# A causal mask added by the vector engine instead of a matmul, a third slot for split weights and six gate buffers

## The chip, the cores and the metric

The kernel runs on one NeuronCore of a Trainium2 chip. A core has a matrix engine (PE in the profile; PEld is its weight load), a vector engine (DVE), a scalar engine (ACT), a second elementwise engine (POOL, GpSimd) and SyncE (SP, which only issues DMAs here). Each engine takes its instructions strictly in the order in which they stand in its stream; between engines there are semaphores. SBUF is the large on-chip memory, PSUM the eight banks into which matmuls write. The metric is the device time of one launch in microseconds (us).

## The reference, cut to what matters

One layer of a streaming encoder: a new stream of 1024 frames ("prompt") and 32 further frames of a running stream ("sample"). The input is normalised and projected to q, k, v, a forget gate, the conv inputs and four gates (ga, gb, ma, mb). One branch is causal softmax attention in 16 heads of 64 channels with a bias from cumulative forget gates, the other a causal depthwise convolution of width 31 with a LayerNorm.

```python
def fox_attend(q, k, v, cq, ck, qpos, kpos):
    s = jnp.einsum('bqhd,bkhd->bhqk', q, k)
    bias = cq[..., None] - ck[:, None, :]              # per head, C = cumsum(log f)
    mask = qpos[:, None] >= kpos[None, :]
    s = jnp.where(mask[None, None], s + bias, jnp.finfo(jnp.float32).min)
    p = jax.nn.softmax(s, axis=-1)
    return jnp.einsum('bhqk,bkhd->bqhd', p, v)

def mixer_outputs(x, o_attn, conv, ga, gb, ma, mb, ...):
    ya = (o_attn * silu(ga)) @ w_pa
    yb = (silu(layernorm(conv, ln_g, ln_b)) * silu(gb)) @ w_pb
    m = sigmoid(ma) * ya + sigmoid(mb) * yb
    return x + m @ w_out
```

A query block is 128 frames, so of its scores only the last 128 columns (the diagonal block) need the mask.

## The kernel before, in words

The 1056 frames (1024 prompt, 32 sample) lie in the free dimension in three chunks of 352 columns. **Weights.** Every projection is done in 128-row output tiles, and with more than one matmul's precision: a 512 KB weight tile `raw` comes from HBM (`load_raw`, L85, issued on SP), ACT rounds it to a high half `wh` (`split_w`, L91), POOL forms the low half `wl = raw - wh` in three pieces (L94), and PE makes three passes per contraction tile, `wh·xh`, `wl·xh`, `wh·xl` (`mms`, L102). `wh` and `wl` have two buffers each; a `raw` buffer is free again when POOL has made `wl` of it.

**Three phases.** Up to about 601 us: transposes and splitting of the input, and the projections ub, ua, v, k, q, ga; the convolution's 31 taps run beside them on DVE (L264). From 601 to about 1090 us: attention, with the projections of the gates gb, ma and mb as filling work for PE. From 1090 us: the projections pa and pb of the two branches and the output projection.

**Order of the work.** PE's stream is in the order of the program's text throughout. Up to the end of the first phase DVE and ACT are too. POOL and SP everywhere, and DVE and ACT from the attention on, are ordered by the framework's scheduler, from its own costs and from the priorities that the text sets (`tc.high_priority`); an engine's order is then fixed in the program. So the number of buffers of a tile and the cost of an added instruction can change the order in these streams.

**Attention.** Sixteen heads of eight query blocks, 128 blocks in all, and four groups of sample queries between them. For block i of a head, `Block.scores` makes 128 x (i+1)·128 scores in one bank (up to 512 columns) or two: per bank a matmul of 128 rows (L931) and one of 68 rows (L932; head channels in split halves and the bias), and at the end of the block's last bank a third one, L934, which multiplies an identity (`identb`, bf16) by the mask (`cmaskb`, 0 and a large negative number, bf16) and so adds the mask to the diagonal block in the same accumulation. Then DVE takes the negated row maximum (L936), ACT makes P = exp(scores - max) with the row sum (L939), DVE the reciprocal of the sum (L941), and POOL scales P (L942). `Block.turn` transposes P on PE in 128 x 128 pieces (L956) and copies them to SBUF, the first four pieces by ACT and the others by DVE (L959). After a head's block 7, `values` multiplies with V. The tile of scores, `psS`, has two buffers of two banks. The loop over blocks n runs: scores of block n+3, turn of block n, `fill(4)` (four contraction tiles, 12 matmuls of 352 columns, of the gates' projections; its evacuation `t` is L763 on ACT, and has one PSUM bank here), values. So the scores of block n+2 wait until the exp of block n has read `psS`.

**After the attention.** `outproj` runs over eight output tiles each of pa, pb and out. For pa, `mk_pa` loads a gate in three chunks `sma` (L1155 on SP, from the pool `sg2` with 4 buffers), takes a tanh (L1156 on ACT), multiplies with the product (DVE) and stores to `s_ya` (L1160 on SP). Beside pa runs the LayerNorm's end for the conv branch, `ln_out`, column by column: loads of y and g (L1110, L1111 on SP), DVE L1112, L1113, ACT silu L1114 and L1115, DVE L1116, ACT L1120 (`c_h`), POOL L1121 (`c_l`).

Of the kernel before, what the change touches and what calls it, by code (L numbers as in the profile page):

```python
# [7 lines left out]

F32 = mybir.dt.float32
F32R = mybir.dt.float32r  # L10
BF16 = mybir.dt.bfloat16
AF = mybir.ActivationFunctionType
ALU = mybir.AluOpType
AX = mybir.AxisListType
# [8 lines left out]
KT = 8  # L23
# [19 lines left out]
C_ID, C_CM, C_SM, C_BO = 0, 128, 256, 288  # L43
# [5 lines left out]
def build(tc, xT, xt, wv, wf, ckT, cv, clT, stT, vec, cst, yT, kT, vO, lfO, cpT, csT):  # L49
    nc = tc.nc  # L50
# [3 lines left out]
    def pool(name, bufs=1, stack=es, **kw):  # L54
        return stack.enter_context(tc.tile_pool(name=name, bufs=bufs, reuse_waits="tile", **kw))
# [15 lines left out]
    cp = pool("cp")  # L71
    wp = pool("wp", 2)
# [5 lines left out]
    def f32(ap):  # L78
        return ap.bitcast(F32)
# [7 lines left out]

    def split_w(raw, offset=2000):
        with tc.high_priority(offset=offset):
            wh = wp.tile([128, KT, 128], F32R, name="wh", tag="wh")  # L90
            nc.scalar.copy(wh, raw)  # L91
            wl = wp.tile([128, KT, 128], F32R, name="wl", tag="wl")
            for k0, k1 in WSP:
                nc.gpsimd.tensor_sub(wl[:, k0:k1, :], raw[:, k0:k1, :], f32(wh[:, k0:k1, :]))  # L94
        return wh, wl
# [40 lines left out]
    def fetch():  # L136

        if plan:
            key = plan.pop(0)
            if not plan:  # L140
                rawp[:] = [wp]
            split[key] = split_v(key[1]) if key[0] == "v" else split_w(load_raw(key))

    def steps(key, rh, rl, pspool, evac):

        w = split.pop(key) if key in split else split_w(load_raw(key))
        for c in range(3):
            ps = pspool.tile([128, CH], F32, name="pj", tag="pj")
            for kt in range(KT):
                mms(ps, w, rh, rl, csl(c), range(kt, kt + 1), kt == 0, kt == KT - 1)  # L150
                beat()
                if (c, kt) == (0, 5) and not split:
                    fetch()
                if kt < KT - 1:
                    yield False
            with tc.high_priority(offset=4000):
                evac(c, csl(c), ps)
            yield True
# [166 lines left out]
    cst_t = xip.tile([128, NCST], F32, name="cst_t")  # L325
# [31 lines left out]
    nc.vector.memset(eps_t, EPS)  # L357
    ident = cp.tile([128, 128], F32, name="ident")
    smask = cp.tile([128, TS], F32, name="smask")
    identb = cp.tile([128, 128], BF16, name="identb")  # L360
    cmaskb = cp.tile([128, 128], BF16, name="cmaskb")
    bones = cp.tile([128, 128], F32R, name="bones", tag="ob")
    qg8 = cp.tile([128, 1], F32, name="qg8")
    qs_t = cp.tile([128, 8, TS], F32, name="qs_t")
# [111 lines left out]

    def consts():
        nc.vector.tensor_copy(smask, cst_t[:, C_SM:C_SM + TS])
        nc.vector.tensor_copy(identb, cst_t[:, C_ID:C_ID + 128])
        nc.vector.tensor_copy(cmaskb, cst_t[:, C_CM:C_CM + 128])  # L480
        nc.vector.tensor_copy(bones, cst_t[:, C_BO:C_BO + 128])
        nc.vector.tensor_scalar(qg8, vec_t[:, V_QG:V_QG + 1], 0.125, None, op0=ALU.mult)

# [85 lines left out]
    for c in range(4):  # L569
# [15 lines left out]
        for t in range(8):  # L585
            ps = pj.tile([128, 512], F32, name="pjv", tag="pj")
            n = 0
            for kt in range(KT):
                sl = slice(t * 128, t * 128 + 128)
                wh, wl = wh2[kt // 4][:, kt % 4, :], wl2[kt // 4][:, kt % 4, :]  # L590
# [213 lines left out]
    last = taps[-KC:]  # L804
# [36 lines left out]
    class Sample:  # L841
# [15 lines left out]
        def scores(self):  # L857
            g, kc, pf = self.g, self.kc, self.pf
            ps = psS.tile([128, 2, 512], F32, name="psS", tag="S")
            for j in range(4):  # L860
                rows = slice(64 * (j % 2), 64 * (j % 2) + 64)
                q = qs_t[rows, 2 * g + j // 2, :]
                nc.tensor.matmul(ps[32 * j:32 * j + 32, 0, :], q, kc[rows, j // 2, :], start=True, stop=True)
                nc.tensor.matmul(ps[32 * j:32 * j + 32, 1, :TS], q, ks_t[rows, 2 * g + j // 2, :],
                                 start=True, stop=True)
            nc.vector.scalar_tensor_tensor(pf[:, :PAST], ps[:, 0, :], cq[:, g:g + 1], pf[:, :PAST],
                                           op0=ALU.add, op1=ALU.subtract)
            nc.vector.scalar_tensor_tensor(pf[:, PAST:], ps[:, 1, :TS], cq[:, g:g + 1], pf[:, PAST:],
                                           op0=ALU.add, op1=ALU.subtract)
            nc.vector.tensor_add(pf[:, PAST:], pf[:, PAST:], smask)  # L870
            nm = ap.tile([128, 3], F32, name="nm", tag="nm", bufs=6)
            nc.vector.tensor_reduce(nm[:, 0:1], pf, axis=AX.X, op=ALU.max, negate=True)
            nc.scalar.activation(pf, pf, AF.Exp, bias=nm[:, 0:1], accum_out=nm[:, 1:2])
            nc.vector.reciprocal(nm[:, 2:3], nm[:, 1:2])
            nc.vector.tensor_scalar(pf, pf, nm[:, 2:3], None, op0=ALU.mult)
# [37 lines left out]
    class Block:  # L913
# [5 lines left out]
        def scores(self):  # L919
            i = self.i  # L920
            QA, QB, KA, KB = self.head.q
            nk = (i + 1) * 128
            qsl = slice(i * 128, i * 128 + 128)
            ps = psS.tile([128, 2, 512], F32, name="psS", tag="S")
            nb = 1 if nk <= 512 else 2
            w = nk // nb
            wm = max(w, 256)
            for b in range(nb):
                last = b == nb - 1
                ksl = slice(b * w, b * w + wm)  # L930
                nc.tensor.matmul(ps[:, b, :wm], QB[:, qsl], KB[:, ksl], start=True, stop=False)  # L931
                nc.tensor.matmul(ps[:, b, :wm], QA[:, qsl], KA[:, ksl], start=False, stop=not last)  # L932
                if last:
                    nc.tensor.matmul(ps[:, b, w - 128:w], identb, cmaskb, start=False, stop=True)  # L934
            nm = ap.tile([128, 3], F32, name="nm", tag="nm", bufs=6)
            nc.vector.tensor_reduce(nm[:, 0:1], ps[:, :nb, :w], axis=AX.XY, op=ALU.max, negate=True)  # L936
            self.P = P = ap.tile([128, T], F32, name="P", tag="P", bufs=3)
            with tc.issue_after(sides["tables"].ins):
                nc.scalar.activation(P[:, :nk].rearrange("p (b w) -> p b w", b=nb), ps[:, :nb, :w], AF.Exp,  # L939
                                     bias=nm[:, 0:1], accum_out=nm[:, 1:2])  # L940
            nc.vector.reciprocal(nm[:, 2:3], nm[:, 1:2])  # L941
            nc.gpsimd.tensor_scalar(P[:, :nk], P[:, :nk], nm[:, 2:3], 1.0, op0=ALU.mult, op1=ALU.mult)  # L942
# [131 lines left out]
    p3 = ExitStack()  # L1074
# [10 lines left out]
            return (pq if self.n % 8 == 0 else pj3).tile(*a, **k)  # L1085

    pjC = Banks3()
    sg2 = pool("sg2", 4, stack=p3, side="right")
    bg = pool("bg", 5, stack=p3, side="right")
    rawp.extend(pool(f"rw{i}", 1, stack=p3, side="right") for i in range(2))  # L1090

# [44 lines left out]
    def outproj(g, rh, rl, mk, between=lambda f: None):  # L1136

        w = split_w(load_raw((g, 0)))
        pss = [pjC.tile([128, CH], F32, name="pj", tag="pj") for _ in range(3)]
        for kt in range(KT):  # L1140
            for c in range(3):
                mms(pss[c], w, rh, rl, csl(c), range(kt, kt + 1), kt == 0, kt == KT - 1)
        ev = mk(0)
        with tc.high_priority(offset=4000):
            for c in range(3):
                ev(c, csl(c), pss[c])
        for f in range(1, 8):
            between(f)
            proj((g, f), rh, rl, pjC, mk(f))
# [128 lines left out]
```

## Time and profile before

| what | value |
|---|---|
| median of 3 runs | 1400.15 us (1399.85 to 1401.89) |
| profiled execution | 1400.09 us, of which the profile's span is 1398.3 us and 1.8 us lie outside it |
| granted TensorE clock | 1.00 (the page's PEclk row has 9, the highest digit, in all 40 slices) |
| busy share of the span | PE 99%, PEld 94%, DVE 60%, POOL 45%, ACT 43% |
| attention, 600 to 1080 us | PE busy 479.1 of 480.0 us, DVE 239.2, ACT 245.9, POOL 188.4 |
| pa, 1080 to 1210 us | PE busy 127.6 of 130.0 us |

A row of the timeline gives an instruction's start in us, its length, its engine, line, operation, `output<-inputs`, and in brackets how long the engine was idle before it and which instruction's end released it. The matrix engine is pipelined: successive matmuls overlap, their ends are modelled, and what a matmul costs is the distance between starts, not the length. Rows with "x2" or "x3" join instructions that follow each other. SPq is SyncE's queue that issues DMAs; its length holds the waiting of the instruction. Groups give busy time, mean length in ns and, behind the bar, the idle time of the engine just before, with what ended it.

### The profile page before, as it was taken

The numbers are of one execution on the slowest core, as the hardware profiler recorded it, in microseconds if no ns is written. First come the engines' busy times: TensorE is split into PE (matmuls) and PEld (weight loads), VectorE is DVE, ScalarE is ACT, GpSimd is POOL, SyncE is SP. The second block draws the span as 40 slices with busy tenths as digits, with TensorE's granted clock in tenths as the row PEclk, the third lists the DMA queues.
The fourth block names the chain that finished last, engine by engine and source line by source line (L and its number), as shares of the span: only waits on it lengthen the run. The fifth ranks groups of instructions, "written<-read, shape, count | busy, mean of one in ns | idle before, by whom it ended". The sixth has DMA issues, their size and how long they took to land.

```text
span 1398.3 us, 24190 instructions
## 1 busy us (share of the span) xinstructions
PE 1386.1 (99%) x9382; PEld 1313.9 (94%) x9382; DVE 835.5 (60%) x1072; ACT 607.0 (43%) x1190; POOL 635.3 (45%) x605
## 2 busy tenths in 40 slices
PE   8999999999999999999999999999999999999998
PEld 7999999999999999998888888888888998999998
DVE  6687787888998999545555655543343594132111
ACT  6322334645464642244454555545544556222100
POOL 2324254555776875444343443332332366254320
PEclk9999999999999999999999999999999999999999
DMA  4242333428342343334545555454542878344431
GB/s 181 93 142 92 120 108 102 159 89 229 98 157 93 127 137 98 133 106 131 143 132 142 152 144 156 112 153 110 167 120 73 302 232 277 120 148 143 143 107 47
DMA packets 110610, 192.81 MB, mean 138 GB/s; under 512 B 33760, under 2 KB 78688, under 8 KB 110496
## 3 DMA queue, kind: packets, MB, share of 16 engines
q1 hardware_dynamic: 110352, 191.21, 43.8%
q8 instruction: 74, 1.21, 0.4%
q14 instruction: 40, 0.33, 0.1%
q10 hardware_dynamic: 144, 0.07, 0.0%
HBM read 125.58 MB, written 65.64 MB: 137 GB/s over the span
## 4 chain that ended last, share of the span: by engine, by line
PE 89%; DVE 4%; DMA 3%; ACT 2%; POOL 1%; issue 1%; SPq 0%; ACTq 0%; DVEq 0%; POOLq 0%
PE pj L102 64%; PE pjv L592 7%; PE po L975 5%; PE ptr L956 5%; PE psS L931 3%; PE psS L932 2%; DMA a<-s_o 1%; PE psS L934 1%; POOL wl L94 1%; DMA s_q<-qh 1%; PE pst L708 1%; DVE y L1112 1%; POOL c_l L1121 1%; DVE y L1113 0%; DVE y L1116 0%
## 5 line engine op out<-in xcount | busy, mean ns | idle before, releaser
L102 PE MATMUL pj<-xh,wh 128*128 128x352 f32 (+2 forms) x1536 | 509.3, 332 | 0.4 <-ACT t L763 0.3
L102 PE MATMUL pj<-xl,wh 128*128 128x352 f32 (+2 forms) x1536 | 494.5, 322 | 0.2
L102 PE MATMUL pj<-xh,wl 128*128 128x352 f32 (+2 forms) x1536 | 493.3, 321 | 0.0
L94 POOL TENSOR_TENSOR wl<-raw,wh 128x384 fp32r<-128x384 f32 (+1 forms) x258 | 328.1, 1300 | 242.8 <-ACT wh L91 216.2
L264 DVE SCALAR_TENSOR_TENSOR y<-u,vec_t,y 128x1086 f32<-128x1086 f32 x240 | 383.7, 1599 | 23.4 <-ACT y L261 19.4
L102 PEld LDWEIGHTS pj<-xh,wh 128*128 128x128 f32 x1536 | 288.6, 188 | 4.3 <-issue 1.2
L102 PEld LDWEIGHTS pj<-xh,wl 128*128 128x128 f32 x1536 | 289.2, 188 | 0.7 <-POOL wl L94 0.5
L102 PEld LDWEIGHTS pj<-xl,wh 128*128 128x128 f32 x1536 | 288.6, 188 | 1.4 <-DVE xl L437 1.4
L942 POOL TENSOR_SCALAR P<-P,nm 128x128 f32<-128x128 f32 (+7 forms) x128 | 108.6, 849 | 229.4 <-DVE nm L941 197.8
L936 DVE TENSOR_REDUCE nm<-psS 128x1 f32<-128x128 f32 (+7 forms) x128 | 96.8, 756 | 97.2 <-PE psS L934 89.3
L91 ACT CAST wh<-raw 128x1024 fp32r<-128x1024 f32 x86 | 90.2, 1049 | 114.7 <-PE pj L102 83.9
L939 ACT ACTIVATE P<-psS,nm 128x128 f32<-128x128 f32 (+7 forms) x128 | 95.4, 745 | 39.8 <-DVE nm L936 39.0
L959 ACT COPY pt<-ptr 128x512 f32<-128x512 f32 (+3 forms) x128 | 65.0, 508 | 102.1 <-PE ptr L956 101.9
L725 POOL TENSOR_TENSOR ql<-qn,qh 128x352 fp32r<-128x352 f32 (+1 forms) x48 | 65.1, 1355 | 74.1 <-ACT qh L724 44.0
L956 PE MATMUL ptr<-ident,P 128*128 128x128 f32 x576 | 84.8, 274 | 0.0
L975 PE MATMUL po<-pt,V 128*64 128x256 f32 x640 | 72.6, 382 | 0.0
L592 PE MATMUL pjv<-vwh,xh 128*128 128x260 f32 x256 | 72.5, 283 | 0.0
L592 PE MATMUL pjv<-vwl,xh 128*128 128x260 f32 x256 | 72.4, 283 | 0.0
L592 PE MATMUL pjv<-vwh,xl 128*128 128x260 f32 x256 | 72.3, 282 | 0.0
L941 DVE RECIPROCAL nm<-nm 128x1 f32<-128x1 f32 x128 | 20.7, 162 | 84.3 <-ACT P L939 83.9
L931 PE MATMUL psS<-KB,QB 128*128 128x256 f32 (+2 forms) x192 | 69.3, 362 | 0.6 <-ACT t L761 0.6
L975 PEld LDWEIGHTS po<-pt,V 128*64 128x64 f32 x640 | 44.5, 137 | 24.2 <-issue 3.0
(208 smaller groups left out, 2304.6 us busy)
## 6 DMA issues: line engine op xcount, KB each, us to landing
raw<-wf SPq DMA_DIRECT2D x88, 512.0 KB
QB<-s_q SPq DMA_DIRECT2D x32, 256.0 KB
KB<-s_k SPq DMA_DIRECT2D x32, 256.0 KB
kT<-qn SPq DMA_DIRECT2D x8, 528.0 KB
s_ga<-t SPq DMA_DIRECT2D x24, 176.0 KB
s_gb<-t SPq DMA_DIRECT2D x24, 176.0 KB
s_ma<-t SPq DMA_DIRECT2D x24, 176.0 KB
s_mb<-t SPq DMA_DIRECT2D x24, 176.0 KB
```

The costliest lines, as they stand in the source:

```text
L91: nc.scalar.copy(wh, raw)
L94: nc.gpsimd.tensor_sub(wl[:, k0:k1, :], raw[:, k0:k1, :], f32(wh[:, k0:k1, :]))
L102: nc.tensor.matmul(ps, a[:, kt, :], b(kt, sl), start=(first and n == 0), stop=(last and n == N - 1))
L264: t = nc.vector.scalar_tensor_tensor(y, u[:, i:i + CW], w, y, op0=ALU.mult, op1=ALU.add)
L592: nc.tensor.matmul(ps[:, :VC], a, b, start=(n == 0), stop=(n == 23))
L725: nc.gpsimd.tensor_sub(ql[:, :n], qn[:, o], f32(qh[:, :n]))
L931: nc.tensor.matmul(ps[:, b, :wm], QB[:, qsl], KB[:, ksl], start=True, stop=False)
L936: nc.vector.tensor_reduce(nm[:, 0:1], ps[:, :nb, :w], axis=AX.XY, op=ALU.max, negate=True)
L939: nc.scalar.activation(P[:, :nk].rearrange("p (b w) -> p b w", b=nb), ps[:, :nb, :w], AF.Exp, bias=nm[:, 0:1], accum_out=nm[:, 1:2])
L942: nc.gpsimd.tensor_scalar(P[:, :nk], P[:, :nk], nm[:, 2:3], 1.0, op0=ALU.mult, op1=ALU.mult)
L956: nc.tensor.transpose(pt[:, 128 * j:128 * j + 128], P[:, 128 * (4 * u + j):128 * (4 * u + j) + 128], ident)
L975: nc.tensor.matmul(po[rows], V[:, j, :], parts[c][:, j, :], start=(c % 2 == 0 and j < 2), stop=(c % 2 == 1 and j >= 2 * c))
```

## The change

The matmul L934 goes, and with it the load of `identb` as weights. In its place a DVE addition of 128 x 128 float32 numbers, from PSUM and an SBUF mask back into the same place of PSUM, stands between the scores' matmuls and the row maximum. `wh` and `wl` have three buffers instead of two, `sg2` six instead of four, and a scratch area that the program doesn't use for its transfers is set to 1024 bytes, which leaves room in SBUF. The two bf16 constants become one float32 tile.

```diff
@@ split_w
-            wh = wp.tile([128, KT, 128], F32R, name="wh", tag="wh")
+            wh = wp.tile([128, KT, 128], F32R, name="wh", tag="wh", bufs=3)
             nc.scalar.copy(wh, raw)
-            wl = wp.tile([128, KT, 128], F32R, name="wl", tag="wl")
+            wl = wp.tile([128, KT, 128], F32R, name="wl", tag="wl", bufs=3)
@@ constants
-    identb = cp.tile([128, 128], BF16, name="identb")
-    cmaskb = cp.tile([128, 128], BF16, name="cmaskb")
+    cmask = cp.tile([128, 128], F32, name="cmask")
...
-        nc.vector.tensor_copy(identb, cst_t[:, C_ID:C_ID + 128])
-        nc.vector.tensor_copy(cmaskb, cst_t[:, C_CM:C_CM + 128])
+        nc.vector.tensor_copy(cmask, cst_t[:, C_CM:C_CM + 128])
@@ Block.scores
-                last = b == nb - 1
                 ksl = slice(b * w, b * w + wm)
                 nc.tensor.matmul(ps[:, b, :wm], QB[:, qsl], KB[:, ksl], start=True, stop=False)
-                nc.tensor.matmul(ps[:, b, :wm], QA[:, qsl], KA[:, ksl], start=False, stop=not last)
-                if last:
-                    nc.tensor.matmul(ps[:, b, w - 128:w], identb, cmaskb, start=False, stop=True)
+                nc.tensor.matmul(ps[:, b, :wm], QA[:, qsl], KA[:, ksl], start=False, stop=True)
+            diag = ps[:, nb - 1, w - 128:w]
+            nc.vector.tensor_add(diag, diag, cmask)
             nm = ap.tile([128, 3], F32, name="nm", tag="nm", bufs=6)
@@ after the attention
-    sg2 = pool("sg2", 4, stack=p3, side="right")
+    sg2 = pool("sg2", 6, stack=p3, side="right")
@@ program
-    nc = _bacc.Bacc("TRN2", target_bir_lowering=False, num_devices=1)
+    nc = _bacc.Bacc("TRN2", target_bir_lowering=False, num_devices=1, dynamic_dma_scratch_size=1024)
```

Lines of the changed kernel are lower by 1 early in the file and by 3 or 4 later (L91 becomes L90, L939 becomes L935, the new addition is L930).

PE's stream loses the 128 matmuls and 128 weight loads of the mask and keeps its order otherwise. The scheduler orders the other streams anew, at three places that matter below.

The first is DVE at block 7 of head 0 and blocks 0 and 1 of head 1; the same stands at the end of most heads. RECIPROCAL is the row sum's reciprocal, COPY a part of a `turn`, SCALAR_TENSOR_TENSOR a tap of the convolution. Before:

```order
L936 TENSOR_REDUCE nm<-psS 128x1
L959 COPY pt<-ptr_6685 128x128
L936 TENSOR_REDUCE nm<-psS 128x1
L941 RECIPROCAL nm<-nm 128x1
L959 COPY pt<-ptr_6719 128x2x128
L264 SCALAR_TENSOR_TENSOR y<-u,vec_t,y 128x1086
L941 RECIPROCAL nm<-nm 128x1
L936 TENSOR_REDUCE nm<-psS 128x1
```

And after the change, at the same place:

```order
L930 TENSOR_TENSOR psS<-psS,cmask 128x128
L955 COPY pt<-ptr_6683 128x128
L932 TENSOR_REDUCE nm<-psS 128x1
L930 TENSOR_TENSOR psS<-psS,cmask 128x128
L932 TENSOR_REDUCE nm<-psS 128x1
L955 COPY pt<-ptr_6717 128x2x128
L263 SCALAR_TENSOR_TENSOR y<-u,vec_t,y 128x1086
L937 RECIPROCAL nm<-nm 128x1 x2
L930 TENSOR_TENSOR psS<-psS,cmask 128x128
L932 TENSOR_REDUCE nm<-psS 128x1
```

The row maximum of block 7 now stands behind a turn's copy, and the reciprocal of block 7 behind the next turn's copy and a tap.

The second place is ACT at the start of the attention: L761 and L758 evacuate the last tiles of the projection ga, L939 and L935 are the exp of blocks 0 and 1, and L763 and L760 evacuate the first chunk of the projection gb. Before:

```order
L761 ACTIVATE t<-pj 128x352 x3
L91 CAST wh<-raw 128x1024
L761 ACTIVATE t<-pj 128x352 x3
L91 CAST wh<-raw 128x1024
L737 ACT_TABLE_LOAD
L939 ACTIVATE P,nm<-psS,nm 128x128
L763 COPY t<-pj 128x352
L939 ACTIVATE P,nm<-psS,nm 128x256
```

And after the change:

```order
L758 ACTIVATE t<-pj 128x352 x2
L90 CAST wh<-raw 128x1024
L758 ACTIVATE t<-pj 128x352
L734 ACT_TABLE_LOAD
L935 ACTIVATE P,nm<-psS,nm 128x128
L90 CAST wh<-raw 128x1024
L760 COPY t<-pj 128x352
L935 ACTIVATE P,nm<-psS,nm 128x256
```

The weights' cast for the next projection but one now stands between the exp of block 0 and the evacuation of gb's first chunk; before it stood after several blocks more. All later casts of the attention stand one projection earlier in the same way, and so do POOL's subtractions.

The third place is ACT from the cast for the fourth tile of pa (the first row in both lists) to the cast for the fifth (the last row). y and g are columns of `ln_out`, and numbers two lower name the same column after the change (y_12590 is y_12588). Before:

```order
L91 CAST wh<-raw 128x1024
L1114 ACTIVATE y_12590<-y_12590,vec_t 128x1056
L1115 ACTIVATE g_12591<-g_12591 128x1056
L1156 ACTIVATE sma<-sma 128x352
L1115 ACTIVATE g_12700<-g_12700 128x1056
L1120 CAST c_h<-y_12590 128x1056
L1114 ACTIVATE y_12699<-y_12699,vec_t 128x1056
L1156 ACTIVATE sma<-sma 128x352
L1120 CAST c_h<-y_12699 128x1056
L1156 ACTIVATE sma<-sma 128x352
L91 CAST wh<-raw 128x1024
```

And after:

```order
L90 CAST wh<-raw 128x1024
L1111 ACTIVATE g_12480<-g_12480 128x1056
L1116 CAST c_h<-y_12468 128x1056
L1110 ACTIVATE y_12479<-y_12479,vec_t 128x1056
L1152 ACTIVATE sma<-sma 128x352 x3
L1116 CAST c_h<-y_12479 128x1056
L1111 ACTIVATE g_12589<-g_12589 128x1056
L1110 ACTIVATE y_12588<-y_12588,vec_t 128x1056
L90 CAST wh<-raw 128x1024
```

The cast for pa's fifth tile has moved up past the rest of one column and nearly all of the next (before, it stood behind `c_h` of y_12699; now it stands behind the silu of y_12588, the column before that one). On SP the loads of `sma` are now issued up to six ahead.

More of the change, by code (lines that the diff above doesn't have):

```diff
@@ L10 @@
 F32R = mybir.dt.float32r
-BF16 = mybir.dt.bfloat16
 AF = mybir.ActivationFunctionType
```

## The prediction

> **What bounds the kernel now.** I read the busy shares first, then the costliest groups, the busy time of the attention stage alone, the timeline of PE around a mask matmul, and last what PE waited for after the attention. The page:
>
> ```profile
> span 1398.3 us, 24190 instructions
> PE 1386.1 (99%) x9382; PEld 1313.9 (94%) x9382; DVE 835.5 (60%) x1072; ACT 607.0 (43%) x1190; POOL 635.3 (45%) x605
> L934 PE MATMUL psS<-cmaskb,identb 128*128 128x128 bf16 x128 | 29.6, 231 | 0.0
> L936 DVE TENSOR_REDUCE nm<-psS 128x1 f32<-128x128 f32 (+7 forms) x128 | 96.8, 756 | 97.2 <-PE psS L934 89.3
> ```
>
> PE is the bound: 99% busy. The third row is a trap: 29.6 us of mask matmuls is overlapping, modelled length. What a matmul costs is the distance to the next start. The last row says that DVE spends 89.3 us idle waiting for a mask matmul, so DVE follows PE here. The stage by itself, and what PE waits for in it (engine, line, releaser: total, times, longest):
>
> ```profile
> 600.00:1080.00 480.00, 479.08 (x3506) 420.52 (x3505) 239.24 (x458) 245.90 (x545) 188.40 (x259) 1.00 0.47 132
> PE psS L931 <- ACT t L761: 0.6, 1, 0.6
> PE pj L102 <- ACT t L763: 0.3, 1, 0.3
> ```
>
> In 480 us PE lacks 0.9. The columns are PE, PEld, DVE, ACT, POOL busy: DVE is at 50%, ACT at 51%. So anything taken from PE's stream here shortens the stage one for one, and anything added to DVE costs only where a chain through DVE comes late for PE.
>
> **The mask matmul.** Two places of PE's timeline:
>
> ```profile
> 705.47 0.33 PE L932 MATMUL psS<-KA,QA 68*128 68x384 f32 x1
> 705.64 0.23 PE L934 MATMUL psS<-cmaskb,identb 128*128 128x128 bf16 x1
> 705.71 0.50 PE L956 MATMUL ptr<-ident,P 128*128 128x128 f32 x3
> ...
> 711.93 0.32 PE L102 MATMUL pj<-xl,wh 128*128 128x352 f32 x1
> 712.10 0.27 PE L908 MATMUL ptr<-ident,oq 128*64 128x128 f32 x1
> ```
>
> From L934's start to the next is 705.71 − 705.64 = 0.07 us; L932 keeps its own 0.17 whatever follows. With 128 of them: 128 × 0.07 = 9.0 us. The rows' last digit allows 0.06 to 0.08, so 7.7 to 10.2. What could eat it is the weight load of the transposes, which then has to hide behind L932. The last two rows show such a pair: a transpose directly behind a float32 matmul starts after 0.17 us, the distance of a matmul of that size, with nothing added. A few mask matmuls stand before something else than a transpose and may be worth less, so I take 8.8, and for the range 0 to 10.2.
>
> [...]
>
> **The addition on DVE.** No row has an addition of 128 columns in PSUM. Nearest are copies out of PSUM and a larger addition with one operand there:
>
> ```profile
> L959 DVE COPY pt<-ptr 128x128 f32<-128x128 f32 x16 | 4.5, 281 | 0.0
> L980 DVE TENSOR_TENSOR ot<-ot,po 64x512 f32<-64x512 f32 x30 | 20.5, 685 | 51.1 <-ACT ot L979 51.1
> ```
>
> The copy has the same size and source, 281 ns; 685 (four times the columns) is the upper bound, and 150 the lower, what a reciprocal of one column takes at 624.49 below. I take 0.28: 128 × 0.28 = 36 us on DVE, which goes from 239 to 275 of 480 busy, and 0.28 more between a block's scores and its row maximum. The first copy of the constants to bf16 is dropped: nothing. [...]
>
> Does the longer chain come late? The next scores need exp to have read its buffer (block n before block n+2), and the turn needs POOL's scaling. Block 7 of head 0, where DVE's new order puts a turn's copy before the row maximum, and copy and tap before the reciprocal:
>
> ```profile
> 621.79 1.22 DVE L936 TENSOR_REDUCE nm<-psS 128x1 f32<-128x1024 f32 x1
> 624.49 0.15 DVE L941 RECIPROCAL nm<-nm 128x1 f32<-128x1 f32 x1
> 625.22 1.78 DVE L264 SCALAR_TENSOR_TENSOR y<-u,vec_t,y 128x1086 f32<-128x1086 f32 x1
> 623.13 1.12 ACT L939 ACTIVATE P<-psS,nm 128x1024 f32<-128x1024 f32 x1 [0.65 <-DVE nm L936]
> 624.74 1.12 POOL L942 TENSOR_SCALAR P<-P,nm 128x1024 f32<-128x1024 f32 x1 [1.27 <-DVE nm L941]
> 626.75 0.28 PE L931 MATMUL psS<-KB,QB 128*128 128x256 f32 x1
> 630.17 0.60 PE L956 MATMUL ptr<-ident,P 128*128 128x128 f32 x4
> ```
>
> exp ends at 624.25, the scores that take its buffer start at 626.75: 2.5 us of room. Needed are the addition (0.28) and the copy (0.28, and up to 0.3 of waiting for its transposes): 0.9, leaving 1.6. POOL ends at 625.86, the turn starts at 630.17: 4.3 of room; the reciprocal now comes after the tap, at 627.0 plus the delay of some 0.6 instead of 624.49, so 3.1 later, leaving 1.2. Both hold. This is the tightest form that recurs from head to head; smaller blocks have 3 us or more. Cost 0.
>
> Singular places are tighter. Each cast of weights stands one projection earlier on ACT; at three blocks it and an evacuation now stand ahead of the exp. The worst, block 5 of head 12:
>
> ```profile
> 977.17 0.90 ACT L939 ACTIVATE P<-psS,nm 128x768 f32<-128x768 f32 x1 [0.61 <-DVE nm L936]
> 978.07 0.44 ACT L763 COPY t<-pj 128x352 f32<-128x352 f32 x1
> 978.40 1.06 ACT L91 CAST wh<-raw 128x1024 fp32r<-128x1024 f32 x1
> 981.04 0.39 PE L931 MATMUL psS<-KB,QB 128*128 128x512 f32 x1
> ```
>
> If the cast ends at 979.46 as before, exp then takes until about 980.4, and 0.6 is left before 981.04. I count nothing, and up to 0.5 for each of three such places.
>
> **The start of the attention.** The cast for the projection after gb's first now stands ahead of gb's first evacuation:
>
> ```profile
> 601.92 2.68 POOL L94 TENSOR_TENSOR wl<-raw,wh 128x384 fp32r<-128x384 f32 x3 [8.76 <-ACT wh L91]
> 604.63 0.33 SPq L85 DMA_DIRECT2D raw<-wf  x1
> DMA  0000000000995329899899999665899743000000
> 605.56 0.45 ACT L763 COPY t<-pj 128x352 f32<-128x352 f32 x1 [1.94 <-issue]
> 606.06 0.43 PE L102 MATMUL pj<-xh,wh 128*128 128x352 f32 x1 [0.28 <-ACT t L763]
> ```
>
> PE waits here already for the evacuation (one PSUM bank). The weight tile's load (604.63) follows POOL's subtraction (to 604.60), which frees the slot. The third row is the DMA engines' busy share in 40 slices of 0.1 us from 604.6: this load and one store are done by 608.4, after 3.8 us, so I estimate 3.3 for the load alone. With the cast before it moved ahead of ga's last evacuation, subtraction and load come about 3 us earlier, the load at some 601.6; with 3.3 us for it and 1.04 for the cast, the evacuation starts near 605.9 instead of 605.56. I take +0.4, from 0 to 1.6.
>
> **pa's tail.** What PE waits for from 1080 us on, and the chain behind the longest of these waits:
>
> ```profile
> PE pj L102 <- POOL wl L94: 2.4, 4, 1.7
> 1144.01 3.76 POOL L94 TENSOR_TENSOR wl<-raw,wh 128x384 fp32r<-128x384 f32 x2
> 1147.80 0.33 SPq L85 DMA_DIRECT2D raw<-wf  x1
> 1148.70 0.91 SPq L1155 DMA_DIRECT2D sma<-s_ma x2
> 1154.55 0.50 ACT L1156 ACTIVATE sma<-sma 128x352 f32<-128x352 f32 x1 [6.07 <-DMA sma<-s_ma]
> 1156.31 1.04 ACT L91 CAST wh<-raw 128x1024 fp32r<-128x1024 f32 x1
> 1158.53 5.78 POOL L94 TENSOR_TENSOR wl<-raw,wh 128x384 fp32r<-128x384 f32 x3
> 1158.69 0.32 PE L102 MATMUL pj<-ah,wh 128*128 128x352 f32 x1
> 1160.67 0.43 PE L102 MATMUL pj<-ah,wl 128*128 128x352 f32 x1 [1.65 <-POOL wl L94]
> ```
>
> A weight load stands on SP until POOL is done at 1147.77; the gates' loads behind it come late; ACT waits 6.07 us for one; the cast behind it comes at 1156.31, the low half after 1158.53, and PE, which reaches that tile at 1158.69, loses 1160.67 − 1158.69 − 0.16 = 1.82 us. All four waits make 2.4 by the first row, and with the restart (1.82 for a wait of 1.65, 0.17 more each) 3.1. After the change that cast stands more than a column of `ln_out` earlier, behind a silu that answers to the one at 1139.80 and gates that were loaded six ahead; its place is then near 1141, 15 us before. So the longest wait, with a shorter one behind it (some 2.3 us), goes. The two others, at tile 6 (0.8), hang on POOL pieces of nearly 2 us each; I count half. Gain 2.7, from 0 to 3.2.
>
> **Sum**, against the profiled execution's 1400.09 (the median of the runs is 0.06 above it, the 1.8 us outside the span are untouched): − 8.8 (mask) − 2.7 (tail) + 0.4 (start) + 0 (first phase, whose PE, DVE and ACT order stands; late chains) = 1389.0.
>
> **The rivals.**
>
> *The chain over DVE comes late (slower).* Room at block 7 is 2.5 us for the buffer. If addition, copy and queueing take more than that, PE stands at each of the 16 heads. To end above 1402.9 it must give back 1402.9 − 1389.0 = 13.9 us, 0.87 a head, so the chain has to grow by 2.5 + 0.87 = 3.4 us, not 0.9. Against: DVE has 205 us idle. For: DVE is in order, and one wrong neighbour (a tap of 1.78 behind a wait) makes such a step. At 3.6 us: 16 × 1.1 = 17.6, 1406.6.
>
> *The tail keeps its waits*, since POOL's pieces (5.78 us for three) and not the cast's place set them: 1389.0 + 2.7 = 1391.7. For: SP, POOL and DMA are reordered, and the DMA there is dense. Against: 15 us of lead.
>
> *The matmul hides what takes its place*: 0.07 is needed anyway for the transposes' weights, so only the tail gains: 1397.8. Against: the pair at 711.93. Half of it, 1393.4, is likelier, where L932 has 256 columns.
>
> *The start and the singular blocks cost all they can*: 1389.0 + 1.2 + 1.5 = 1391.7.
>
> **How the numbers follow.** The forecast (1387.0 to 1390.5) gets 0.52, the tail or the singular places 0.22 together (up to 1393), the matmul's room wholly or partly lost 0.11 (1393 to 1397.8), the late chain 0.10, a larger gain 0.05 (10.2 and 3.2 without the start's cost: 1386.7). What differs by 0.2%, 2.8 us, is about the least that a measurement of this kernel can tell from no change: faster is under 1397.3. Of the lost room a third lies above that, so same 0.04; slower 0.09, the late chain but for its smallest forms; faster 0.87. The range 1386.5 to 1395.5 leaves out the late chain and the worst part of the lost room, some 0.16.
>
> **What would show it.** Right: L932 to L956 at 0.12 to 0.24 with no third matmul; the DVE addition near 0.28 us, 36 us in all; 9 us less between the first scores and the last; no wait over 0.5 us for `psS` or `P`; the cast of pa's fifth tile near PE's third tile, and the sum of PE's waits for `wl` under 1. Wrong: PE idle before L931 behind ACT's exp at the heads' ends, L956 starting 0.07 late, or PE idle on `wl` in pa as long as now.

## The result, and the profile after

The changed kernel takes 1392.7 us (median of 6 runs, 1391.74 to 1393.33) against 1400.04 (median of 6, 1399.54 to 1401.89): a ratio of 0.9946, interval 0.9933 to 0.9958. It is faster by 7.3 us; 11.1 were forecast. The profiled execution, the longest of the six, took 1393.33 us, with a span of 1391.5.

The page of the changed kernel: span, busy times, the chain's shares, and three groups (the addition, the row maximum, the exp).

```profile
span 1391.5 us, 24013 instructions
PE 1379.1 (99%) x9254; PEld 1318.7 (95%) x9254; DVE 865.1 (62%) x1199; ACT 604.4 (43%) x1190; POOL 636.8 (46%) x605
PE 96%; DVE 1%; ACT 1%; POOL 0%; issue 0%; DMA 0%; SPq 0%; ACTq 0%; DVEq 0%; POOLq 0%
L935 ACT ACTIVATE P<-psS,nm 128x128 f32<-128x128 f32 (+7 forms) x128 | 95.2, 744 | 67.1 <-DVE nm L932 57.5
L932 DVE TENSOR_REDUCE nm<-psS 128x1 f32<-128x128 f32 (+7 forms) x128 | 96.8, 756 | 9.5 <-DVE psS L930 0.5
L930 DVE TENSOR_TENSOR psS<-psS,cmask 128x128 f32<-128x128 f32 x128 | 38.0, 297 | 89.9 <-PE psS L928 89.0
```

The addition takes 297 ns, and DVE's idle time now stands ahead of it. ACT's idle time ahead of exp has grown from 39.8 to 67.1 us, 57.5 of them on the row maximum: the chain is longer, as it had to be. The stages, in the same columns as before, and then what PE waited for from 598 us to the end:

```profile
600.00:1080.00 480.00, 476.37 (x3398) 428.30 (x3397) 270.11 (x587) 244.23 (x546) 189.28 (x262) 1.00 0.48 133
600.00:612.00 12.00, 9.50 (x49) 8.82 (x48) 5.01 (x11) 4.07 (x8) 7.90 (x8) 0.86 0.24 79
1080.00:1210.00 130.00, 130.00 (x818) 128.10 (x817) 70.77 (x70) 65.59 (x81) 65.61 (x41) 1.00 0.73 246
PE pj L101 <- ACT t L760: 2.6, 2, 1.9
PE psS L927 <- ACT t L758: 0.6, 1, 0.6
```

pa has no wait left: PE is busy in all of its 130 us. The attention has lost time: PE idles 3.6 of 480 us there where it idled 0.9, and in the stretch from 600 to 612 us the granted clock is 0.86.

PE's stream is the same in both kernels but for the mask, so each instruction's start can be set beside its counterpart's, and the differences of the distances add up to the change of the whole. For the two profiled executions, 1393.33 and 1400.09, this gives:

| where | us | forecast |
|---|---|---|
| 128 mask matmuls | - 8.6 | - 8.8 |
| pa's tail | - 3.7 | - 2.7 |
| stall at the start of the attention | + 1.6 | + 0.4 |
| low clock behind it | + 1.5 | none |
| PE waiting for an evacuation `t`, after the turns | + 3.1 | 0 |
| the rest | - 0.6 | 0 |
| sum | - 6.7 | - 11.1 |

**The mask.** Where L934 stood, PE goes from the scores straight to the transposes:

```profile
707.31 0.34 PE L927 MATMUL psS<-KB,QB 128*128 128x384 f32 x1
707.49 0.34 PE L928 MATMUL psS<-KA,QA 68*128 68x384 f32 x1
707.66 0.49 PE L952 MATMUL ptr<-ident,P 128*128 128x128 f32 x3
```

0.17 us from L928 to L952, the distance that L932 had to L934; the transposes' weight load adds nothing here.

**The start.** ACT, SP and PE at the beginning of the attention:

```profile
605.88 1.04 ACT L90 CAST wh<-raw 128x1024 fp32r<-128x1024 f32 x1 [3.16 <-DMA raw<-wf]
606.83 0.45 ACT L760 COPY t<-pj 128x352 f32<-128x352 f32 x1
602.34 0.33 SPq L84 DMA_DIRECT2D raw<-wf  x1
607.32 0.43 PE L101 MATMUL pj<-xh,wh 128*128 128x352 f32 x1 [1.90 <-ACT t L760]
607.59 0.32 PE L101 MATMUL pj<-xh,wl 128*128 128x352 f32 x1
...
609.34 0.49 PE L101 MATMUL pj<-xh,wh 128*128 128x352 f32 x1
609.64 0.49 PE L101 MATMUL pj<-xh,wl 128*128 128x352 f32 x1
```

The load is issued at 602.34 and its tile is there at 605.88; the cast waits for it 3.16 us, and the evacuation, on which PE waits, stands behind the cast. PE is idle for 1.90 us instead of 0.28. About a microsecond after it resumes, its matmuls come 0.30 us apart instead of 0.16: from 608.28 to 611.69 the granted clock is 0.50. This costs 1.5 us in all.

**The evacuations.** The longest of PE's new waits inside the attention, at the end of head 1, with DVE, ACT and PE:

```profile
651.77 1.33 DVE L263 SCALAR_TENSOR_TENSOR y<-u,vec_t,y 128x1086 f32<-128x1086 f32 x1
653.02 0.29 DVE L930 TENSOR_TENSOR psS<-psS,cmask 128x128 f32<-128x128 f32 x1
653.22 0.28 DVE L955 COPY pt<-ptr 128x128 f32<-128x128 f32 x1
653.42 1.22 DVE L932 TENSOR_REDUCE nm<-psS 128x1 f32<-128x1024 f32 x1
654.76 1.11 ACT L935 ACTIVATE P<-psS,nm 128x1024 f32<-128x1024 f32 x1 [1.46 <-PE pj L101]
655.86 0.44 ACT L760 COPY t<-pj 128x352 f32<-128x352 f32 x1
656.36 0.43 PE L101 MATMUL pj<-xh,wh 128*128 128x352 f32 x1 [0.75 <-ACT t L760]
```

ACT's stream has the exp of block 7 ahead of the evacuation. The exp comes late, so the evacuation comes late, and PE has one PSUM bank for these projections. The profile puts ACT's wait down to PE; the exp starts when DVE's row maximum, L932, has ended (654.64).

**pa.** The cast for the fifth tile is the first row; before, it stood at 1156.31. The two others are the start of that tile on PE, where the longest wait was; its passes with `wh` and `wl` are now 0.16 us apart:

```profile
1135.82 1.03 ACT L90 CAST wh<-raw 128x1024 fp32r<-128x1024 f32 x1
1155.66 0.32 PE L101 MATMUL pj<-ah,wh 128*128 128x352 f32 x1
1155.82 0.32 PE L101 MATMUL pj<-ah,wl 128*128 128x352 f32 x1
```

### The profile page after: what moved, and what is told of

It reads as the page before. It is cut to its first block, busy times and chain, and to the rows that moved or that the text cites. A ratio compares the mean times of both kernels' runs of the same rounds, so it can differ in the third digit from the quotient of the medians.

```text
span 1391.5 us, 24013 instructions
## 1 busy us (share of the span) xinstructions
PE 1379.1 (99%) x9254; PEld 1318.7 (95%) x9254; DVE 865.1 (62%) x1199; ACT 604.4 (43%) x1190; POOL 636.8 (46%) x605
## 4 chain that ended last, share of the span: by engine, by line
PE 96%; DVE 1%; ACT 1%; POOL 0%; issue 0%; DMA 0%; SPq 0%; ACTq 0%; DVEq 0%; POOLq 0%
PE pj L101 71%; PE pjv L589 7%; PE po L971 5%; PE ptr L952 5%; PE psS L927 3%; PE psS L928 2%; PE pst L705 1%; PE pst L704 1%; PE ptx L432 0%; DMA xtok<-xt 0%; ACT xh L434 0%; POOL wl L93 0%; PE pjs L546 0%; DVE xl L435 0%; PE psS L860 0%
## 5 line engine op out<-in xcount | busy, mean ns | idle before, releaser
L93 POOL TENSOR_TENSOR wl<-raw,wh 128x384 fp32r<-128x384 f32 (+1 forms) x258 | 333.3, 1319 | 234.0 <-ACT wh L90 190.0
L90 ACT CAST wh<-raw 128x1024 fp32r<-128x1024 f32 x86 | 90.0, 1047 | 83.1 <-PE pj L101 78.2
L935 ACT ACTIVATE P<-psS,nm 128x128 f32<-128x128 f32 (+7 forms) x128 | 95.2, 744 | 67.1 <-DVE nm L932 57.5
L932 DVE TENSOR_REDUCE nm<-psS 128x1 f32<-128x128 f32 (+7 forms) x128 | 96.8, 756 | 9.5 <-DVE psS L930 0.5
L930 DVE TENSOR_TENSOR psS<-psS,cmask 128x128 f32<-128x128 f32 x128 | 38.0, 297 | 89.9 <-PE psS L928 89.0
L952 PE MATMUL ptr<-ident,P 128*128 128x128 f32 x576 | 84.2, 272 | 0.0
L952 PEld LDWEIGHTS ptr<-ident,P 128*128 128x128 f32 x576 | 69.2, 141 | 5.3
```

What stands on the lines that cost most here:

```text
L952: nc.tensor.transpose(pt[:, 128 * j:128 * j + 128], P[:, 128 * (4 * u + j):128 * (4 * u + j) + 128], ident)
```

## The experiments

Runs that were compared ran on the same chip beside runs of the kernel before, whose medians there were 1400.83 us (the first four runs), 1400.37 (start_fix, red_first, both_fix, no_mask) and 1399.56 (the other four); the ratios are to these. Between kernels that lie 1 or 2 us apart the intervals overlap; there the rows of the traces decide, not the totals.

### The mask alone, and the buffers alone

`mask_only` is the changed kernel without the new buffers; the other three are the kernel before with new buffers, all with the smaller scratch area.

```diff
 mask_only:     wh, wl bufs=3 -> 2;  sg2 6 -> 4      (from the changed kernel)
 slots_only:    wh, wl bufs=2 -> 3;  sg2 4 -> 6      (from the kernel before)
 weights_only:  wh, wl bufs=2 -> 3
 gates_only:    sg2 4 -> 6
```

> The mask by DVE alone, two slots for the weights' halves and four gate buffers as before. Theory A (the 128 matmuls give 8.6 us, the longer chain over DVE takes some 3 back at the evacuations behind exp, and the loss at the start of the attention and the gain in pa belong to the buffers): 1400.0 - 8.6 + 2.9 = 1394.3. Rival B (the small waits in the attention come from the weights' casts that the third slot moves, not from the addition): 1391.4. In the profile: A has PE waiting about 0.25 us for the evacuation t once in most heads, B has none beyond those of the kernel before; both have no stall at 605 us and a clock of 1.000.

> The mask stays a matmul; three slots and six gate buffers. Theory A: a stall of about 1.5 us more at the start of the attention, up to 1.7 more from a lowered clock behind it, and 3.7 gained in pa: 1400.0 + 1.5 to 3.2 - 3.7 = 1397.8 to 1399.5. Rival B (the start's loss needs the addition too): 1396.3.

> The mask stays a matmul, four gate buffers; only the third slot for the weights' halves. Theory A (in pa both are needed: the third slot moves the cast, the gate buffers free SP's queue and ACT): start + 1.5 to 3.2, pa 0 to - 2: 1400 to 1403. Rival B (the third slot alone clears pa): 1397.8 to 1399.5.

> The mask stays a matmul, two slots; only six gate buffers. Theory A (the cast still waits for the slot): 1400.0 less 0 to 1.8, no stall at the start. Rival B (the gate buffers alone clear pa, since it was the late gate that held ACT): 1396.3.

| kernel | us | ratio, interval |
|---|---|---|
| mask_only | 1394.21 | 0.9953 (0.9940 to 0.9965) |
| slots_only | 1398.51 | 0.9982 (0.9973 to 0.9991) |
| weights_only | 1397.91 | 0.9979 (0.9970 to 0.9988) |
| gates_only | 1397.01 | 0.9972 (0.9962 to 0.9983) |

What PE waits for from 598 us on, in mask_only, slots_only, weights_only and gates_only, one fence each. The wait of 0.6 us ahead of the first scores, the last row of the first fence, stands in the other three and in the kernel before as well:

```profile
PE pj L101 <- POOL wl L93: 2.4, 2, 2.1
PE pj L101 <- ACT t L760: 1.1, 2, 0.7
PE psS L927 <- ACT t L758: 0.6, 1, 0.6
```

```profile
PE pj L102 <- ACT t L763: 1.9, 1, 1.9
```

```profile
PE pj L102 <- ACT t L763: 1.5, 1, 1.5
```

```profile
PE pj L102 <- POOL wl L94: 0.4, 1, 0.4
PE pj L102 <- ACT t L763: 0.3, 1, 0.3
```

The waits for `t` inside the attention come with the mask: added up on PE as in the table above they are 3.0 us in mask_only and under 0.05 in the other three, so rival B for that run falls. In pa mask_only keeps its 2.4 us, the longest wait standing one tile later. The stall at the start comes with the third slot (slots_only, weights_only) and with nothing else; Theory A holds for slots_only, by this stall more than by its time. In pa it fell twice, for weights_only and for gates_only: either part alone clears the waits, the third slot wholly and the gate buffers but for 0.4 us. They don't add up. The smaller scratch area was never tried alone, but in gates_only PE's distances from 600 us on differ from the kernel before by nothing but the 3.0 us gained in pa. Of the clock mask_only's expectation was wrong too: there the low clock shows at another place, in the first 25 us of that execution (gates_only's has a mean of 0.93 there too, and the kernel before 1.00).

```profile
0.00:25.00 25.00, 21.91 (x129) 19.73 (x129) 15.81 (x40) 16.09 (x36) 7.53 (x15) 0.93 0.79 295
```

### The start, and the order on DVE

`start_fix` holds the cast behind gb's first evacuation, with a dependency that only sets the order on ACT. `red_first` does the same on DVE: a turn's copy stays behind the last row maximum. `both_fix` has both.

```diff
+ cast = nc.scalar.copy(wh, raw)            # start_fix: the cast for gb's third tile
+ tc.add_manual_dep(cast.ins, first_t.ins.name, NoSync)
...
+ sides["red"] = nc.vector.tensor_reduce(nm[:, 0:1], ...)      # red_first
+ if u: tc.add_manual_dep(cpy.ins, sides["red"].ins.name, NoSync)
```

> The changed kernel, with the cast for the projection after gb's first held behind gb's first evacuation. Theory (the moved cast makes the stall at 605 us, and the stall makes the stretch of half clock behind it): 1392.7 - 1.5 to 3.2 = 1389.5 to 1391.2, a granted clock of 1.00 in all runs. Rival (the cast is late anyway and stalls something else, or the clock falls for another reason): 1392.7, clock under 1.000 in some runs.

> The changed kernel, with the turn's copies on DVE held behind the last row maximum issued (as they stood before the change). Theory (the exp of block 7 comes late by addition plus copy, and the evacuation behind it holds PE): the waits for the evacuation shrink from some 3 us to about 1, 1392.7 - 2 = 1390.7. Rival (the addition alone makes exp late, the copy adds nothing): 1392.2 to 1392.9.

> Both orders together. If both theories hold: 1392.7 - 2.5 - 2 = 1388.2; if only the start's: 1390.2; if neither: 1392.7.

start_fix took 1390.91 us (0.9931, 0.9918 to 0.9943), red_first 1392.66 (0.9944, 0.9931 to 0.9956), both_fix 1390.13 (0.9924, 0.9911 to 0.9938). In start_fix the stall is gone, and the waits of head 1 stay. The cast now waits for the load behind the evacuation:

```profile
605.10 0.45 ACT L767 COPY t<-pj 128x352 f32<-128x352 f32 x1 [2.53 <-issue]
605.82 1.05 ACT L90 CAST wh<-raw 128x1024 fp32r<-128x1024 f32 x1 [0.26 <-DMA raw<-wf]
```

Not all of it is gained: between 610 and 612 us PE loses 0.6 us against the kernel before, at the scores of 610.73 and at the projection behind the next turn. The start theory holds for the stall. For the low clock it holds only as far as no stretch of it follows in this execution (1.00 from 600 to 612 us): a single run of start_fix too has a mean clock of 0.998, which the page doesn't place.

red_first fell. The rival was right, and its rows say why:

```profile
653.03 0.29 DVE L930 TENSOR_TENSOR psS<-psS,cmask 128x128 f32<-128x128 f32 x1
653.43 1.23 DVE L932 TENSOR_REDUCE nm<-psS 128x1 f32<-128x1024 f32 x1
654.57 0.28 DVE L955 COPY pt<-ptr 128x128 f32<-128x128 f32 x1
654.77 1.12 ACT L935 ACTIVATE P<-psS,nm 128x1024 f32<-128x1024 f32 x1 [1.46 <-PE pj L101]
```

Without the copy between them the row maximum still starts 0.40 us after the addition's start, exactly as with it; in 95 of the 128 blocks of the changed kernel this distance is 0.38 to 0.40, and in none under 0.32. The copy, which doesn't read the addition's result, started 0.20 us after it at head 1 of the changed kernel, and stood in the gap for nothing. So the price on the chain is 0.40 and not the 0.297 of the addition's row. both_fix agrees with its forecast for the case that only the start's order matters (1390.2).

### The mask left out, and the addition made longer

`no_mask` takes the addition away, and with it the mask, so its attention also sees later frames; `mask_wide` makes it longer by putting 128 columns of zeros ahead of the mask.

```diff
- nc.vector.tensor_add(diag, diag, cmask)                       # no_mask
...
+ mw = min(w, 256)                                              # mask_wide
+ diag = ps[:, nb - 1, w - mw:w]
+ nc.vector.tensor_add(diag, diag, cmask[:, 256 - mw:])
```

> The changed kernel with the mask left out: neither matmul nor addition, so the scores above the diagonal stay in (the attention's result is another). It prices the addition's chain. Theory (the addition costs about 3 us by late evacuations): 1392.7 - 3 = 1389.7, with the stall at the start unchanged. Rival (the addition is hidden, the evacuations are late for another reason): 1392.7.

> The changed kernel with the addition over 256 columns (128 zeros and the mask) instead of 128 where a block has them: some 0.13 us longer, a little more of the same. Theory (the addition's length sets the wait for t): the waits of 0.28 us at six heads' ends become about 0.41, the longest 1.03 about 1.3, PE's waits in the attention 1 to 1.5 us more, 1393.7 to 1394.2. Rival (the order of ACT sets them): as before, 1392.7.

no_mask took 1392.01 us (0.9938, 0.9925 to 0.9950), mask_wide 1392.98 (0.9951, 0.9937 to 0.9965). Both totals lie nearer to their rivals; by their ratios, set against the 1400.04 of the kernel before, they would be 1391.4 and 1393.2, about half-way. But the scheduler orders DVE and ACT anew in both, and the low clock from 600 to 612 us came in no_mask's profiled execution too. So the place has to be looked at, not the total. One of the six heads' ends where the wait is regular: six transposes, then the first matmul into the bank that `t` frees. Before, after, in mask_wide and in no_mask:

```profile
682.15 0.83 PE L956 MATMUL ptr<-ident,P 128*128 128x128 f32 x6
682.73 0.41 PE L102 MATMUL pj<-xh,wh 128*128 128x352 f32 x1
```

```profile
684.13 0.82 PE L952 MATMUL ptr<-ident,P 128*128 128x128 f32 x6
684.96 0.43 PE L101 MATMUL pj<-xh,wh 128*128 128x352 f32 x1
```

```profile
681.59 0.82 PE L954 MATMUL ptr<-ident,P 128*128 128x128 f32 x6
682.55 0.43 PE L101 MATMUL pj<-xh,wh 128*128 128x352 f32 x1
```

```profile
684.66 0.82 PE L951 MATMUL ptr<-ident,P 128*128 128x128 f32 x6
685.23 0.41 PE L101 MATMUL pj<-xh,wh 128*128 128x352 f32 x1
```

0.58, 0.83, 0.96 and 0.57 us. With the addition the wait is 0.25; with one longer by 0.134 (431 ns in its group against 297) it grows by 0.13; without it, it is gone. That is the addition's own doing, at six heads' ends (1.5 us in all). The sum of these waits in no_mask is 1.5 and not 0, so half of the 3.1 us has other causes, which the theory lacked. Most of it moves with the order: in mask_wide the long wait of head 1 is not there, and in no_mask one of 0.84 us stands at another head's end. But 0.5 us comes neither from the addition nor from the order. At the turn of block 0 in seven heads PE starts its next projection 0.05 us after the end of `t` in all three kernels (725.52 us before, 727.24 after, 727.35 in no_mask is the first of them). So PE waited for ACT there before the change too, and the 0.07 us that the mask's matmul gave up became a longer wait for `t`.

```profile
L932 DVE TENSOR_TENSOR psS<-psS,cmask 128x256 f32<-128x256 f32 x112 | 48.2, 431 | 60.7 <-PE psS L929 60.2
```

### The exp behind the evacuation

If PE waits for `t` and `t` waits behind an exp, then the exp of block 7 may go behind `t`. `exp_late` does this on top of start_fix; `mask_gates` has the mask and the gate buffers with two slots only; `mask_gates_late` is that with the late exp.

```diff
+ def soft():                       # exp, reciprocal, scaling of a block
+     x = nc.scalar.activation(P, ps, AF.Exp, ...)
+     if i == 7: tc.add_manual_dep(x.ins, last_t.ins.name, NoSync)
...
  b.turn()
  fill(4 if b.i > 2 or b.head.h != 8 else 0)
+ if seq[n + 3] is a block 7: seq[n + 3].soft()       # else within scores()
```

> The changed kernel with the cast at the start held back as in start_fix, and with the exp of every head's block 7 put behind the gate evacuation t that PE waits for. Theory (PE's waits in the attention are for t, which stands behind an exp that the addition makes late): the waits for t in the attention fall from 3.1 us to under 0.6, 1390.9 - 2.5 = 1388.4. Rival (the late exp then holds the scores' buffer or the turn): 1390.9 or more, with PE waiting at the scores or the transposes.

> The mask by DVE and six gate buffers, but two slots for the weights' halves. Theory (the third slot brings only the loss at the start, since either part alone clears most of pa): 1392.7 - 1.5 - 0 to 1.5 + 0.6 = 1390.3 to 1391.8. Rival (the third slot is needed in pa once the mask is moved, as in mask_only): 1394.

> mask_gates with the exp of block 7 behind the evacuation, as in exp_late. If both theories hold: 1391.1 - 2.5 = 1388.6; if the exp's place does nothing: 1391.1.

| kernel | us | ratio, interval |
|---|---|---|
| exp_late | 1388.43 | 0.9920 (0.9907 to 0.9934) |
| mask_gates | 1390.11 | 0.9932 (0.9920 to 0.9945) |
| mask_gates_late | 1388.80 | 0.9926 (0.9912 to 0.9939) |

exp_late at the same place of head 1, and PE at the regular place:

```profile
652.22 0.45 ACT L767 COPY t<-pj 128x352 f32<-128x352 f32 x1 [1.44 <-PE pj L108]
652.57 1.12 ACT L946 ACTIVATE P<-psS,nm 128x1024 f32<-128x1024 f32 x1
680.58 0.82 PE L972 MATMUL ptr<-ident,P 128*128 128x128 f32 x6
681.15 0.41 PE L108 MATMUL pj<-xh,wh 128*128 128x352 f32 x1
```

The exp starts 0.35 us after the evacuation's start, PE's distance is 0.57, and the waits after the turns add up to 0.8 us more than in the kernel before instead of 3.1, a little above the 0.6 of the forecast; 0.5 of that are the seven blocks above. Behind the start of the attention (past 612 us) nothing waits at the scores or the turns: the rival fell. The same order in mask_gates_late takes these waits from 3.1 to 0.7, and its time lies at the forecast of 1388.6. exp_late and mask_gates_late are the fastest here, and can't be told apart. mask_gates took 1390.11: with the gate buffers, the third slot brings little (pa gains 3.6 us without it and 3.7 with it), and it alone brings the stall at the start.

## Why the prediction was right, and where it was off

Right: the sign, the range (1386.5 to 1395.5) and the bound. The mask matmul was worth its distance of 0.07 and not its 0.23 of length: 8.6 us against 8.8. The transposes' weight load added nothing to the 0.17 us from L928 to L952; that rival falls, half of it too. The addition is 0.297 us, 38 us on DVE, against 0.28 and 36. The late chain did not make the kernel slower; the scores' buffer and the turns had the room that was worked out: from 598 us on no row of PE's waits names an exp or POOL's scaling, and the three singular blocks cost nothing.

That the time lies in the range is in part luck. The band with the most weight, 1387.0 to 1390.5, was missed, and the time lies where the tail or the singular places were to put it. It came there by another way: the tail gave more than forecast and the singular places cost nothing, while waits for an evacuation that had no term, and the stall with its low clock, cost more.

Off by 3.7 us, in three terms:

- *"This is the tightest form that recurs from head to head; smaller blocks have 3 us or more. Cost 0."* The room was worked out for the scores' buffer and for the turn, the two things that need the block's own result. What is queued behind the exp on ACT was left out: the evacuation `t`, for which PE waited 0.13 us at the ends of heads 0 and 1 already, and as long or longer at block 0 of seven heads. It cost 3.1 us. mask_wide and no_mask show the addition's share, about half; exp_late shows that `t`'s place behind the exp is the cause of most of it. The other 0.5 us is a limit of *"anything taken from PE's stream here shortens the stage one for one"*: at those seven blocks it did not.
- The chain was taken to grow by 0.28 and by a copy. It grows by 0.40, the distance from the addition's start to the row maximum that reads its result, and the copy costs nothing (red_first).
- *"I take +0.4, from 0 to 1.6."* The stall's mechanism was right and its size was not: the load came at 602.34, not 601.6, the cast began 3.5 us after it instead of 3.3, and the evacuation started at 606.83 instead of 605.9. The stall cost 1.6 us, the upper end. The low clock behind it was in no term.

In the other direction pa gave 3.7 instead of 2.7: the first group of waits was worth 2.7 us where 2.3 were forecast, and the second went wholly, 1.0 where half of 0.8 was counted. The mechanism was read too narrowly as well. It was told as a chain through the gates' loads and the cast; weights_only clears it without more gate buffers and gates_only nearly without the slot, so each link of that chain was enough to break it.

How much of the low clock is in the median of the six runs can't be told: two of them have a mean clock of 1.000 (1391.74 and 1392.16 us), four of 0.998 or 0.999 (1392.46 to 1393.33). But the two still lie 2.7 and 3.2 us above the forecast, so the low clock is the smaller part of what was missed.

## What to carry to other kernels

When an operation is moved to another engine, follow not only who needs its result but also what is queued behind each waiting instruction on every engine of the chain: here most of the cost inside the attention came from an evacuation that has nothing to do with the mask, behind an exp whose chain had grown by 0.4 us. Price a dependent operation by the distance to the instruction that reads its result, not by its length (0.40 us against 0.297 for this addition). A deeper buffer lets a scheduler put an operation earlier, also ahead of something urgent and before its data is there; look at the first use after a stage's border.

## What the runs showed of the hardware that was not expected

In the profiled execution of the changed kernel a stall of 1.90 us on PE was followed by a stretch of 3.4 us (608.28 to 611.69) with matmuls 0.30 us apart instead of 0.16 and a granted clock of 0.50. In no_mask's the stall was 1.9 us too, and the mean clock from 600 to 612 us was 0.86 as in the changed kernel. In those of red_first and slots_only, with the same stall of 1.9 us, that mean was 1.00:

```profile
600.00:612.00 12.00, 9.47 (x58) 8.85 (x58) 4.67 (x10) 5.12 (x9) 7.51 (x7) 1.00 0.22 74
```

This is red_first; weights_only, with a stall of 1.5 us, has 1.00 there too. In the kernel before, PE's longest wait from 598 us on is 1.65 us, in pa, and the mean clock from 1158 to 1170 us, around it and behind it, is 1.00. So the length of the stall alone does not tell whether a slow stretch follows: 1.9 us came with one in two executions and without one in two others. The start of the kernel agrees: in the first 25 us the mean clock is 0.93 in mask_only and gates_only and 1.00 in slots_only and red_first, with PE busy for 21.9, 21.7, 21.9 and 21.2 us.

In the changed kernel the granted clock falls once more, to 0.50, at 1389.93, 2.1 us after the end of PE's last matmul. What decides when it falls was not shown, and no run moved the stall alone to find out.
